# Two transformer blocks in one kernel: the list scheduler places by its timeline simulator

## The chip, the cores and the metric

The kernel runs on one core of a Trainium2 chip. The metric is the device time of one execution in microseconds (us); the time before is the median of three runs.

## The reference

A sequence of 512 tokens of width 1024 goes through a first block and then, with 16 meta tokens put in front (528 tokens), through a second block of two layers. All is fp32.

- First block: `h = rms_norm(x)`, a projection `h @ w_in`, three kinds of attention on it (banded with dilations 1, 4 and 16; a sliding window with sinks; stick-breaking), three gated branches merged and `@ w_out`, a residual; then `gelu(conv(h @ w_up)[gate]) * conv(h @ w_up)[value] @ w_down` with 4096 hidden columns, a residual.
- Second block, twice: `h += 0.5 * swiglu(rmsnorm(h))` with 2816 hidden columns; a mixer of four retention heads and four differential attention heads (softmax in blocks of 128 queries), `@ w_out`; `h += 0.5 * swiglu(rmsnorm(h))` again. At the end a norm, and the 512 tokens go out.

## The kernel before

**Products.** Every large product is made of three matmuls for one: weights and activations are split into a high part (fp32r, `H`) and a rest (`L`), and `H*yH + H*yL + L*yH` is added up in PSUM (`gemm`, L172; `gemm_pairs`, L206; `v_direct`, L579). The blocks of gate and up weights go through seven half-size products instead of eight (`strassen`, L276 for a product that opens a PSUM bank, L278 for one that adds to it).

**Weights.** A raw block of 128 x 1024 (512 KB) comes by a DMA from SP's queue (`wraw`, L153, three buffers). ACT casts it to the high part and DVE subtracts (`wsplit`):

```python
self.nc.scalar.copy(out=H, in_=raw)
self.nc.vector.tensor_sub(out=L, in0=raw, in1=H.bitcast(F32))
```

(L139 and L140) into `wqH` and `wqL`, four buffers of 1024 columns each. So a weight goes raw buffer, ACT, DVE, TensorE, and each step waits until its buffer is free. For the seven products DVE makes sums of the raw quarters first (L258 to L263).

**Stages.** In the profiled execution, by the code's order: norm, attention A and C (to about 240 and 380 us), attention B with the gate products, the merge of the branches (`merge`, L933 to L937; its 24 gate tiles are read back from DRAM by DMAs on ACT's queue; to about 515), `w_out` and the norms (to 575), the convolution FFN (to about 1030), then the second block: swiglu (to 1490), mixer (to 1720 with `w_out`), swiglu, swiglu of the second layer (to 2525), mixer (to 2740), last swiglu (to 3119), the end.

**Attention steps.** A softmax goes TensorE, DVE, ACT, TensorE, ACT, TensorE: scores (in the mixer L1467 to L1470), maximum on DVE (L1472, L1477), exponent on ACT (L1479), normalization on DVE, transposes on TensorE (L1497, L1501), their copies on ACT (L1498, L1502), products with V (L1504, L1505). `diff_heads` staggers three such blocks by Python generators.

**What sets the order.** The kernel's Python code issues instructions in an order of its own, the program order, and opens pools of tiles with fixed numbers of buffers. When the `TileContext` closes, a list scheduler walks through a simulated time: whenever an engine (or a DMA queue) is free in it, that engine is given the instruction that is earliest in program order among those whose inputs and buffers are ready at that simulated time. Each engine then executes its list strictly in order on the chip, with semaphores wherever one engine needs another's result. Counted in the built program, TensorE's 21,605 matmul instructions follow program order except at 852 places, which all lie in the attention, merge and norm stages; in the long feed-forward stretches there is none. DVE's and ACT's lists interleave evacuations of PSUM with weight splits nearly everywhere.

## Time and profile before

| | |
|---|---|
| median of 3 runs | 3139.04 us (3138.15 to 3143.01) |
| the profiled execution, its own time | 3133.03 us |
| its span, first to last instruction | 3131.2 us |
| TensorE busy | 3101.2 us, 99% |
| DVE busy, ACT busy | 2250.4 us, 72%; 1534.7 us, 49% |
| mean granted clock of TensorE | 0.996 |

The profiled execution lies 6.0 us under the median, and its own time is 1.8 us over its span. A matmul's record is longer than its share of the array (records of neighbours overlap), so the pace of a stretch is its length over its count, and not the mean of the records.

### The profile page before, as it was taken

How to read it: one execution, taken by the hardware profiler on the slowest of the kernel's cores; microseconds unless marked ns; L12 is line 12 of the kernel's file. 1: busy time of each engine (PE TensorE's matmuls, PEld its weight loads, DVE VectorE, ACT ScalarE, POOL GpSimd, SP SyncE). 2: the span in 40 equal slices, each digit the busy share in tenths (PEclk: the TensorE clock that was granted, in tenths of full speed). 3: DMA queues.
4: the chain of work that ended last, by engine and by line, in shares of the span. 5: the costliest groups of instructions: out<-in, count | busy, mean ns of one | idle time of the engine just before them, and what ended most of it. 6: DMA issues, size and time to landing. Idle time of an engine off the chain costs nothing.

```text
span 3131.2 us, 54851 instructions
## 1 busy us (share of the span) xinstructions
PE 3101.2 (99%) x22264; PEld 2869.7 (92%) x22264; DVE 2250.4 (72%) x4225; ACT 1534.7 (49%) x2968; POOL 30.9 (1%) x64
## 2 busy tenths in 40 slices
PE   8999999999999999999999999999999999999998
PEld 6876798989898999999889999999999988899998
DVE  6256677977878887775866877768777586687775
ACT  5346556655555554444643544444444464354443
POOL 1000000000000000000000000000000000000000
PEclk9999999999999999999999999999999999999999
DMA  6121256323233422332112232322323311223232
GB/s 212 60 66 60 89 166 202 105 88 102 101 108 101 135 78 93 102 118 87 52 55 78 82 102 89 101 95 95 102 94 111 100 58 62 71 82 108 95 108 75
DMA packets 96958, 304.41 MB, mean 97 GB/s; under 512 B 12199, under 2 KB 20799, under 8 KB 96576
## 3 DMA queue, kind: packets, MB, share of 16 engines
q1 hardware_dynamic: 90384, 286.63, 27.8%
q0 software_dynamic: 2720, 7.78, 0.8%
q10 hardware_dynamic: 3600, 6.49, 0.7%
q8 instruction: 174, 2.85, 0.4%
q14 instruction: 80, 0.66, 0.1%
HBM read 290.34 MB, written 14.45 MB: 97 GB/s over the span
## 4 chain that ended last, share of the span: by engine, by line
PE 95%; DMA 2%; DVE 1%; ACT 1%; issue 0%; ACTq 0%; SPq 0%; DVEq 0%
PE ps_g L172 35%; PE ps_g L278 18%; PE ps_g L276 9%; PE ps_s L172 8%; PE ps_g L206 7%; PE ps_o L276 5%; PE ps_g L579 2%; PE ps_o L206 1%; DMA tmp_p<-gates 1%; PE ps_s L1468 1%; PE ps_s L513 1%; PE ps_o L535 1%; PE ps_s L1525 1%; PE ps_o L1504 1%; PE ps_o L1534 1%; PE ps_t L494 1%
## 5 line engine op out<-in xcount | busy, mean ns | idle before, releaser
L140 DVE TENSOR_TENSOR wqL<-wraw,wqH 128x512 fp32r<-128x512 f32 (+1 forms) x676 | 604.9, 910 | 278.2 <-ACT wqH L139 270.7
L139 ACT CAST wqH<-wraw 128x512 fp32r<-128x512 f32 (+1 forms) x676 | 527.1, 796 | 511.2 <-PE ps_g L172 282.5
L172 PE MATMUL ps_g<-yL,wqH 128*128 128x264 f32 (+2 forms) x1520 | 429.7, 320 | 0.4 <-DVE yL L414 0.4
L172 PE MATMUL ps_g<-yH,wqH 128*128 128x264 f32 (+2 forms) x1520 | 429.6, 321 | 0.0
L172 PE MATMUL ps_g<-yH,wqL 128*128 128x264 f32 (+2 forms) x1520 | 429.0, 321 | 0.3 <-DVE wqL L140 0.2
L278 PE MATMUL ps_g<-t,wqH 128*128 128x256 f32 (+1 forms) x1760 | 326.5, 283 | 0.0
L172 PEld LDWEIGHTS ps_g<-yL,wqH 128*128 128x128 f32 x1520 | 264.1, 189 | 23.7 <-issue 4.2
L172 PEld LDWEIGHTS ps_g<-yH,wqH 128*128 128x128 f32 x1520 | 262.6, 189 | 21.6 <-issue 3.1
L172 PEld LDWEIGHTS ps_g<-yH,wqL 128*128 128x128 f32 x1520 | 262.4, 189 | 21.0 <-issue 2.6
L278 PEld LDWEIGHTS ps_g<-t,wqH 128*128 128x128 f32 x1760 | 272.3, 188 | 1.8
L278 PE MATMUL ps_g<-t,wqL 128*128 128x256 f32 (+1 forms) x880 | 248.4, 282 | 0.0
L139 ACT CAST wqH<-ws 128x1024 fp32r<-128x1024 f32 x100 | 105.2, 1052 | 126.4 <-PE ps_o L276 33.6
L278 PEld LDWEIGHTS ps_g<-t,wqL 128*128 128x128 f32 x880 | 165.9, 189 | 0.0
L276 PE MATMUL ps_g<-t,wqH 128*128 128x264 f32 (+1 forms) x800 | 148.5, 283 | 0.0
L172 PE MATMUL ps_s<-hL,wqH 128*128 128x264 f32 (+1 forms) x544 | 141.2, 317 | 0.0
L172 PE MATMUL ps_g<-hL,wqH 128*128 128x264 f32 (+1 forms) x544 | 141.2, 317 | 0.0
L172 PE MATMUL ps_g<-hH,wqL 128*128 128x264 f32 (+1 forms) x544 | 141.1, 317 | 0.0
L172 PE MATMUL ps_s<-hH,wqL 128*128 128x264 f32 (+1 forms) x544 | 141.1, 317 | 0.0
L172 PE MATMUL ps_g<-hH,wqH 128*128 128x264 f32 (+1 forms) x544 | 141.0, 317 | 0.0
L172 PE MATMUL ps_s<-hH,wqH 128*128 128x264 f32 (+1 forms) x544 | 140.9, 316 | 0.0
L258 DVE TENSOR_TENSOR ws<-wraw 128x512 f32<-128x512 f32 x100 | 69.2, 692 | 86.1 <-DMA wraw<-in_ffn_w_gate 34.8
L140 DVE TENSOR_TENSOR wqL<-ws,wqH 128x1024 fp32r<-128x1024 f32 x100 | 122.4, 1224 | 6.3 <-ACT wqH L139 2.6
(445 smaller groups left out, 8234.8 us busy)
## 6 DMA issues: line engine op xcount, KB each, us to landing
wraw<-in_ffn_w_gate SPq DMA_DIRECT2D x88, 512.0 KB, 3.6
wraw<-in_ffn_w_up SPq DMA_DIRECT2D x88, 512.0 KB, 3.6
wraw<-in_ffn_w_down SPq DMA_DIRECT2D x88, 512.0 KB, 3.5
wraw<-in_w_in SPq DMA_DIRECT2D x86, 512.0 KB, 3.7
wraw<-in_w_up SPq DMA_DIRECT2D x64, 512.0 KB, 3.7
wraw<-in_w_down SPq DMA_DIRECT2D x32, 512.0 KB, 3.5
wraw<-in_w_gate SPq DMA_DIRECT2D x24, 512.0 KB, 4.1
tmp_p<-gates ACTq DMA_DIRECT2D x24, 256.0 KB, 3.3
```

What stands on the lines that cost most here:

```text
L139: self.nc.scalar.copy(out=H, in_=raw)
L140: self.nc.vector.tensor_sub(out=L, in0=raw, in1=H.bitcast(F32))
L172: self.nc.tensor.matmul(t[:, :m], lhsT=a, rhs=b[:, o:o + m], start=(k == 0 and i == 0), stop=(k == nk - 1 and i == 2))
L206: self.nc.tensor.matmul(q[:, :m], lhsT=a, rhs=b[:, o:o + m], start=(k == 0 and i == 0), stop=(k == nk - 1 and i == 2))
L258: nc.vector.tensor_add(out=S[:, :512], in0=A21, in1=A22)
L276: nc.tensor.matmul(ps, lhsT=a, rhs=b, start=first, stop=last)
L278: nc.tensor.matmul(ps, lhsT=a, rhs=b, start=False, stop=last, skip_group_check=True)
L494: nc.tensor.transpose(pt[:, s * P:(s + 1) * P], p[:, s * P:(s + 1) * P], self.ident)
L513: nc.tensor.matmul(ps[:, c], lhsT=q[:, i * P:(i + 1) * P], rhs=k[:, lo * P:(i + 1) * P], start=True, stop=True)
L535: nc.tensor.matmul(ops[obase:obase + 64, i * P:(i + 1) * P], lhsT=V(kb), rhs=pT[:, s0:s0 + P], start=(kb == lo), stop=(kb == i))
L579: nc.tensor.matmul(ps[:, :256], lhsT=a[:, ts], rhs=w, start=(k == 0 and i == 0), stop=(k == KD - 1 and i == 2))
L1468: nc.tensor.matmul(ps[:nq, :e - a], lhsT=qm[r], rhs=k[2][r, a:e], start=False, stop=not dg)
```

## The change

The scheduler's simulated time comes from another machine model. So far it was a simple model of each instruction's duration; now it is the library's timeline simulator, which follows each engine's parts, queues and transfers event by event. The rule of the list scheduler, the instructions, the numbers of buffers and the transfers stay; what can differ is the order of each engine's list and, with it, which instruction gets which buffer and when a transfer is issued.

```diff
-    with tile.TileContext(nc) as tc:
+    with tile.TileContext(nc, schedule_with_timeline_sim=True) as tc:
         build(tc, A)
```

## Rows read from the trace of the kernel before

**Rows 1.** Busy time of the engines over the whole span, from the page.
```profile
PE 3101.2 (99%) x22264; PEld 2869.7 (92%) x22264; DVE 2250.4 (72%) x4225; ACT 1534.7 (49%) x2968; POOL 30.9 (1%) x64
```

**Rows 2.** Busy time by stage: length; PE, PEld, DVE, ACT, POOL; clock, DMA share, GB/s.
```profile
0.00:8.36 8.36, 0.00 (x0) 0.00 (x0) 1.93 (x10) 3.19 (x5) 2.37 (x9) 1.00 0.72 218
...
38.17:60.00 21.83, 17.66 (x111) 16.02 (x111) 11.61 (x17) 8.96 (x19) 2.48 (x5) 0.84 0.70 246
60.00:240.00 180.00, 179.67 (x885) 138.73 (x886) 68.66 (x98) 74.56 (x175) 12.68 (x25) 0.97 0.20 63
240.00:455.00 215.00, 213.30 (x1271) 171.32 (x1270) 153.45 (x375) 122.45 (x271) 8.50 (x16) 1.00 0.31 100
455.00:575.00 120.00, 116.44 (x788) 106.52 (x787) 86.28 (x174) 68.83 (x139) 0.00 (x0) 1.00 0.59 188
575.00:1490.00 915.00, 914.72 (x6667) 868.58 (x6665) 716.77 (x1179) 471.55 (x786) 0.00 (x0) 1.00 0.30 100
1490.00:1720.00 230.00, 228.77 (x1671) 202.64 (x1671) 158.82 (x460) 111.24 (x307) 0.00 (x0) 1.00 0.18 61
1720.00:2525.00 805.00, 804.62 (x6569) 800.87 (x6568) 594.08 (x1007) 374.91 (x654) 0.00 (x0) 1.00 0.30 97
2525.00:2740.00 215.00, 214.97 (x1381) 181.49 (x1380) 146.71 (x395) 102.68 (x269) 0.00 (x0) 1.00 0.19 62
2740.00:3119.00 379.00, 378.43 (x2800) 359.62 (x2799) 282.22 (x459) 174.42 (x308) 0.00 (x0) 1.00 0.29 94
3119.00:3131.20 12.20, 2.79 (x16) 2.21 (x15) 4.51 (x12) 1.05 (x3) 0.00 (x0) 0.62 0.25 86
```

**Rows 3.** Waits of TensorE over the span: total us, times, longest.
```profile
PE ps_g L172 <- ACT oH L323: 8.4, 1, 8.4
PE ps_g L579 <- DVE qk L563: 4.2, 1, 4.2
PE ps_g L206 <- DVE tmp_p L937: 2.4, 3, 1.1
PE ps_s L1467 <- ACT tmp_P L1479: 0.3, 1, 0.3
```

**Rows 4.** Two pieces of the chain that ended last: start, us, count.
```profile
614.71 5.55 PE ps_g L172 x24
...
1810.13 5.82 PE ps_g L278 x48
```

**Rows 5.** One period of the convolution FFN and one of a swiglu, columns as Rows 2.
```profile
610.45:673.82 63.37, 63.37 (x398) 56.93 (x398) 51.30 (x76) 37.96 (x59) 0.00 (x0) 1.00 0.31 102
...
1801.36:1833.48 32.12, 32.12 (x266) 32.12 (x266) 23.96 (x37) 14.29 (x23) 0.00 (x0) 1.00 0.25 83
```

**Rows 6.** Timeline of a swiglu: one weight split and its later use.
```profile
1799.86 1.06 ACT L139 CAST wqH<-ws 128x1024 fp32r<-128x1024 f32 x1 [0.16 <-PE ps_o L276]
...
1800.98 1.22 DVE L140 TENSOR_TENSOR wqL<-ws,wqH 128x1024 fp32r<-128x1024 f32 x1
...
1808.50 0.40 PE L276 MATMUL ps_g<-t,wqH 128*128 128x264 f32 x2
```

**Rows 7.** TensorE in two stretches at a lower granted clock: length, busy (count), clock.
```profile
40.00:50.00 10.00, 7.65 (x30) 0.66 0.87 296
...
205.00:215.00 10.00, 10.00 (x21) 0.56 0.17 54
```

**Rows 8.** Timeline of TensorE in the second of them.
```profile
207.07 3.78 PE L791 MATMUL ps_s<-rows,sel 4*128 4x512 f32 x4
```

**Rows 9.** Groups of instructions on ACT in the mixers' softmax.
```profile
L1479 ACT ACTIVATE tmp_P<-ps_s,sm 128x264 f32<-128x264 f32 (+4 forms) x88 | 40.3, 460 | 28.5 <-DVE sm L1477 23.3 <-DVE sm L1485 4.2 <-PE ps_s L1470 0.5
...
L1502 ACT COPY tmp_aT<-ps_o 16x128 f32<-16x128 f32 (+1 forms) x36 | 8.5, 236 | 3.1 <-PE ps_o L1501 2.9
```

**Rows 10.** The merge's transfers: queue, count, KB, us to landing.
```profile
tmp_p<-gates ACTq DMA_DIRECT2D x24, 256.0 KB, 3.3
```

**Rows 11.** Weight loads of `gemm` on TensorE, one group of three alike.
```profile
L172 PEld LDWEIGHTS ps_g<-yL,wqH 128*128 128x128 f32 x1520 | 264.1, 189 | 23.7 <-issue 4.2
```

## The prediction

> **What bounds the kernel now.** I read the page's busy times first, then the same times cut into stages, then TensorE's waits, then the chain's pieces for the pace. TensorE is busy 3101.2 of 3131.2 us [rows 1], so 30.0 us of the span are all that it ever stands idle. The stages say where [rows 2]: 8.4 us before the first matmul, 4.2 us in the stretch from 38 to 60, 0.3 + 1.7 + 1.2 + 0.0 = 3.3 us in the four attention stretches (60 to 240, 240 to 455, 1490 to 1720, 2525 to 2740), 3.6 us in merge and `w_out` (455 to 575), 0.3 + 0.4 + 0.6 = 1.2 us in the three feed-forward stretches, 9.4 us in the last 12.2 us: together 30.1, rounded. The named waits are the same ones [rows 3]: the first matmul on the first split input (8.4), the first V product on an evacuation (4.2), the merge on its gate products (2.4), and of all the softmax steps of the mixers one wait of 0.3 us.
>
> A busy TensorE can still be slow, so I check the pace. A 264-column matmul takes 5.82 / 48 = 0.1213 us and a 512-column one 5.55 / 24 = 0.231 us in stretches that nothing interrupts [rows 4]. A swiglu period holds 266 matmuls in 32.12 us, or 0.1208 each [rows 5]: by the code 2 x 84 matmuls of the seven products and 2 x 48 of the down projection, 264 x 0.1213 = 32.0 us. So the feed-forward stretches, 915 + 805 + 379 = 2099 us [rows 2], run at the pace of the instruction, with nothing between, and an order cannot make a matmul shorter.
>
> **The change part by part.** Nothing is added or removed; every engine keeps its instructions. So the cost is what the new lists do to TensorE's idle time and to its clock, stage by stage, against the profiled execution's own 3133.03 us.
>
> *Feed-forward stretches, 2099 us.* TensorE's list here is program order already, and always has a ready matmul, so I expect the same list. What may move is DVE's and ACT's mix of evacuations and weight splits. The cover is the lead of the splits: a buffer is freed by TensorE at 1799.7 (the cast starts 0.16 us later), the split is complete at 1800.98 + 1.22 = 1802.2, and its first matmul starts at 1808.5 [rows 6]: 6.3 us ahead, five DVE splits of 1.22 us. A swap of neighbours on DVE costs an evacuation of some 0.4 us or a split of 1.2 us; neither reaches 6.3. DVE itself is busy 51.3 of 63.4 us in the tightest period [rows 5], so 12 us of waits per period would have to be added before it set the pace. Cost 0; bounds -1.2 (all idle gone) and, if the cover went, +1 us for each of the 7 convolution periods of 63.4 us, +7.
>
> *Start, 8.4 us.* The DMA engines are busy 0.72 of it at 218 GB/s [rows 2], for x and the first weights, and SP's list is short here: one raw block more ahead of x would cost 512 KB / 218 GB/s = 2.4 us, one fewer would give back as much. Taken: 0; bounds -2.4 and +2.4.
>
> *38 to 60 us.* [...] Taken: -1; bounds -7.6 and, if it is no better placed and the wait doubles, +4.2.
>
> *Attention stretches, 840 us.* Here TensorE's list is the scheduler's own work: it fills the time of each softmax with matmuls of neighbouring products, and so well that 3.3 us are left. The gain is bounded by these 3.3 us and one clock drop: over 205 to 215 the clock reads 0.56 [rows 7], 8.8 us at half speed, up to 4.4 us lost, while TensorE worked on L791, matmuls of only 4 rows, near 0.9 us each (3.78 / 4) [rows 8]. Another spacing of these twelve might avoid it, or lengthen it. The loss has more room. The mixers have 36 softmax blocks (the copy x36), and where ACT stood idle before the exponent it mostly waited for DVE's scaled maximum, 23.3 us over 88 exponents [rows 9], or 0.26 each. TensorE hides all that today. If the new list puts its filling matmuls earlier, and a third of the blocks (12) then leaves TensorE waiting for two exponents of 0.46 us and two such idles of 0.26, that is 12 x 1.4 = 17 us; all 36 give 52. I take a tenth of the blocks, 4 x 1.4 = +6, nearer the row of today's single wait of 0.3 us [rows 3] than the far end; bounds -7.7 and +52.
>
> *Merge and `w_out`.* ACT's queue issues the 24 gate loads of 3.3 us each [rows 10], behind whatever ACT executes; the sigmoid, DVE's product and the freeing of a PSUM bank wait for each. Three waits of TensorE come of it now [rows 3]. Twice as many would be +2.4; none, with the norm's gaps closed too, -3.6. Taken: 0.
>
> *The end, 9.4 us idle.* It is a dependent chain from the last matmul over sum, norm and the last output transfers; no order shortens it. Cost 0.
>
> Sum: 0 + 0 - 1 + 6 + 0 + 0 = +5 on 3133.03, so 3138 for an execution like the profiled one; against the median, which lies 6.0 us higher, 3139.04 + 5 = 3144 us. I do not trust the sign of a sum of -1 and +6, but the place of the largest term I do.
>
> The TensorE's clock, told by rows: it fell to half once behind the idle 4.2 us and once under the 4-row matmuls. [...]
>
> **The rivals.**
>
> *Slower, by uncovered softmax blocks.* A third to all of the 36 blocks, as priced: +17 to +52, that is 3156 to 3191 us. For it: TensorE's list in these 840 us is remade by the change, and the present one leaves nothing to gain. Against it: ACT is busy 49% and DVE 72%, so a product's matmuls are nearly always there to fill with, and the mixers' one wait shows how much cover there is. It decides from about 9 uncovered blocks on.
>
> *Faster, by gaps and clock.* The 4.2 us wait, both clock drops, and half of the small gaps of attention and merge: 4.2 + 3.4 + 4.4 + 3.5 = 15.5, so 3123.5 us. For it: each of these hangs on one place in a list, and the new model follows queues and transfers. Against it: several must fall together to be seen at all.
>
> *Faster, by hidden stalls.* TensorE's loads are busy only 138.7 + 171.3 + 202.6 + 181.5 = 694 of the 840 us of attention [rows 2]. If that meant that TensorE stalls inside its records there, up to 146 us could be won, 2993 us. Against it: a load takes 189 ns [rows 11], and behind a 512-column matmul that paces at 231 ns [rows 4] it fills only 82% of a saturated stretch; 82% of 840 us are 689, just what is read. [...]
>
> *No change of any order that matters.* Program order decides ties in both models; if readiness falls alike, all lists are nearly the same and the time is 3139.
>
> **How the numbers follow.** 0.2% (6.3 us) is about what a measurement of this kernel can tell from no change. My own case, small gaps traded in the attention stretches (-6 to +10 us; 3133 to 3149), holds 0.44, and 0.33 of it lies within 0.2%, 0.11 above. Lists that change nothing 0.08, all within. Uncovered softmax blocks 0.27, all slower. Faster by gaps and clock 0.19, faster by hidden stalls 0.02: 0.21. So faster 0.21, same 0.41, slower 0.38. For eight in ten I go from the middle of the faster case down to the bounds without the start, 3139 - 1.2 - 7.6 - 7.7 - 3.6 = 3119, to the upper rival without its last quarter, 3183. My likeliest case alone is 3133 to 3149.
>
> **What would show it.** Right: TensorE busy within 10 us of 3101, the swiglu period at 32.1 us with 266 matmuls, the first wait near 8.4 us, differences only in rows of 38 to 60, attention and merge. The step on attention is wrong if waits of L1467, L1497 or L1504 on ACT or DVE add up to more than 10 us, or if those stretches get shorter by more than 8. The step on the feed-forward stretches is wrong if a period is longer than 32.1 or 63.4 us or if TensorE waits for `wqL`. The forecast as a whole is wrong if DVE's list puts evacuations of later products ahead of splits for 6 us or more, or if SP's queue stands behind a buffer that is freed later than before.

## The result, and the profile after

The changed kernel takes 3263.86 us (median of 4 runs, 3260.58 to 3267.16), against 3138.6 us for the kernel before in the same comparison (3137.31 to 3143.01): a ratio of 1.0397, 95% interval 1.0379 to 1.0415. It is 125 us slower, and the predicted range ended at 3183 us.

The profiled execution of the changed kernel took 3265.32 us. Its page's busy times, as [rows 1]:

```profile
PE 3174.3 (97%) x22264; PEld 2924.9 (90%) x22264; DVE 2243.5 (69%) x4225; ACT 1548.7 (47%) x2976; POOL 31.0 (1%) x64
```

The span is 3263.5 us, 132.3 longer (more than the 125 of the medians, because the profiled execution before lay 6.0 us under its median). Of these, 59.2 are new idle time of TensorE (3263.5 - 3174.3 = 89.2, before 30.0), and 73.1 are more time recorded as busy, for the same 22264 instructions. DVE's and ACT's work is what it was to within 1%.

To compare stages I cut the trace after where TensorE has started as many matmuls as at the cuts of [rows 2]. Length; PE, PEld, DVE, ACT, POOL; clock, DMA share, GB/s:

```profile
8.36:53.15 44.79, 44.47 (x233) 35.54 (x233) 35.24 (x57) 28.24 (x49) 6.36 (x12) 1.00 0.70 242
53.15:233.66 180.51, 177.46 (x886) 141.14 (x884) 68.18 (x98) 68.24 (x167) 13.78 (x27) 0.97 0.24 77
233.66:500.41 266.75, 234.80 (x1272) 186.04 (x1270) 153.34 (x382) 130.10 (x287) 8.51 (x16) 0.88 0.25 80
500.41:624.86 124.45, 119.67 (x789) 108.78 (x788) 84.79 (x167) 67.02 (x136) 0.00 (x0) 0.97 0.56 185
624.86:1561.29 936.43, 922.47 (x6666) 875.65 (x6665) 717.71 (x1185) 474.98 (x789) 0.00 (x0) 0.99 0.30 98
1561.29:1823.37 262.08, 255.22 (x1672) 219.77 (x1671) 162.10 (x460) 115.51 (x309) 0.00 (x0) 0.87 0.16 53
1823.37:2628.94 805.57, 805.05 (x6568) 801.80 (x6567) 585.73 (x1004) 379.09 (x658) 0.00 (x0) 1.00 0.30 97
2628.94:2872.26 243.32, 234.25 (x1381) 194.49 (x1379) 149.63 (x395) 104.36 (x268) 0.00 (x0) 0.89 0.17 55
2872.26:3251.41 379.15, 378.24 (x2801) 359.55 (x2800) 280.17 (x462) 177.20 (x310) 0.00 (x0) 1.00 0.29 94
```

Three stages carry the loss: the first block's attention from 240 us (266.75 against 215, +51.8), mixer 0 (+32.1) and mixer 1 (+28.3). The stage of the convolution FFN is +21.4, merge and `w_out` +4.5. The second stretch of swiglu is +0.6 and the last one +0.2; the stretch up to the 232nd matmul is 6.9 us shorter.

Each of the two mixers now holds one stretch of time at half clock that has no counterpart before, and the first block's attention holds a third:

```profile
394.00:435.00 41.00, 30.83 (x118) 23.47 (x119) 16.56 (x76) 16.36 (x54) 0.00 (x0) 0.50 0.13 42
1647.00:1715.00 68.00, 62.48 (x215) 43.14 (x215) 35.03 (x138) 29.74 (x110) 0.00 (x0) 0.50 0.02 8
2711.00:2760.00 49.00, 44.59 (x145) 29.19 (x143) 22.13 (x78) 18.13 (x69) 0.00 (x0) 0.51 0.00 1
```

In mixer 0 TensorE makes 215 matmuls in 68 us, 0.32 us each, at a granted clock of 0.50 throughout. DVE is busy half of it, and the DMA engines almost never (0.02): hardly any weight is being used. The product matmuls (L172 alone) of mixer 0 after show why; length, PE, PEld, clock, DMA share, GB/s:

```profile
1570.00:1580.00 10.00, 8.91 (x65) 8.17 (x65) 1.00 0.32 107
1580.00:1590.00 10.00, 8.56 (x63) 7.98 (x64) 1.00 0.04 11
...
1640.00:1650.00 10.00, 3.18 (x20) 2.37 (x18) 0.83 0.31 106
1650.00:1660.00 10.00, 0.00 (x0) 0.00 (x0) 0.50 0.00 1
...
1700.00:1710.00 10.00, 0.00 (x0) 0.00 (x0) 0.50 0.00 0
1715.00:1725.00 10.00, 9.63 (x79) 9.37 (x77) 1.00 0.03 6
```

The same view of the kernel before, in its mixer 0:

```profile
1510.00:1520.00 10.00, 6.94 (x44) 5.74 (x45) 1.00 0.16 50
...
1560.00:1570.00 10.00, 5.32 (x28) 3.90 (x29) 1.00 0.23 85
1580.00:1590.00 10.00, 5.62 (x30) 4.21 (x31) 1.00 0.00 1
1600.00:1610.00 10.00, 9.68 (x78) 9.51 (x79) 1.00 0.11 36
```

Before, 28 to 44 product matmuls per 10 us were spread among the softmax steps as long as these lasted, and 78 came once they were over. After, more than 60 come at the start, and then the softmax steps stand alone. What the clock does to one of them, the product with V: duration in ns, least, median, most, before and then after.

```profile
L1504 PE MATMUL ps_o<-vh,tmp_aT x160: 271/275/377, 1505.7 to 2619.1; 128*128 128x128 f32 x160
```
```profile
L1504 PE MATMUL ps_o<-vh,tmp_aT x160: 270/418/583, 1596.0 to 2758.6; 128*128 128x128 f32 x160
```

After, the 40 of them that start from 1663.6 to 1703.3 us, at a clock of 0.50, have a median of 421 ns, and the 25 from 2645.2 to 2699.9 us, at 1.00, a median of 275.

TensorE's waits after, as [rows 3]: total us, times, longest.

```profile
PE ps_g L172 <- ACT oH L323: 8.7, 1, 8.7
PE ps_o L535 <- ACT tmp_pT L497: 7.6, 10, 1.1
PE ps_s L904 <- issue: 6.7, 1, 6.7
PE ps_s L904 <- DVE ca L901: 6.3, 1, 6.3
PE ps_t L1426 <- ACT vh L1427: 6.1, 4, 2.3
PE ps_s L364 <- DVE rc L353: 3.9, 5, 1.5
```

But for the first, which stood there before, they are steps of attention and norm, many and short; none of TensorE's waits in this view is for a DMA. The named waits explain only part of the loss, because 73 of the 132 us are recorded as busy and are not gaps.

The steady periods of the convolution FFN and of swiglu, found in the trace after by matmul count, as [rows 5]:

```profile
729.12:792.24 63.12, 63.12 (x398) 56.81 (x397) 51.79 (x78) 32.93 (x50) 0.00 (x0) 1.00 0.30 97
1904.64:1936.76 32.12, 32.12 (x266) 32.12 (x265) 24.13 (x38) 14.37 (x24) 0.00 (x0) 1.00 0.29 96
```

The swiglu period is as long as before, and the steady period of the convolution FFN is 0.25 us shorter for the same matmuls (63.12 against 63.37). The 21.4 us of that stage lie elsewhere: the matmuls fall 5 us behind over the first 25 us of it (625 to 650), and another 17 between 1084 and 1191, around the norm that ends the convolution FFN. TensorE's named waits in those 107 us add up to 10.5 us, the longest for the last hidden activations (`hH`, L1092, 3.7 us) and for the split output of the norm (`yL` and `yH`, L413 and L414, 3.3 us).

### The profile page after: what moved, and what is told of

The parts are those of the page before. It is cut to its first block, busy times and chain, and to the rows that moved or that the text cites. A ratio compares the mean times of both kernels' runs of the same rounds, so it can differ in the third digit from the quotient of the medians.

```text
span 3263.5 us, 54955 instructions
## 1 busy us (share of the span) xinstructions
PE 3174.3 (97%) x22264; PEld 2924.9 (90%) x22264; DVE 2243.5 (69%) x4225; ACT 1548.7 (47%) x2976; POOL 31.0 (1%) x64
## 4 chain that ended last, share of the span: by engine, by line
PE 93%; DVE 2%; ACT 2%; DMA 1%; issue 1%; DVEq 0%; ACTq 0%; SPq 0%
PE ps_g L172 35%; PE ps_g L278 18%; PE ps_g L276 9%; PE ps_s L172 8%; PE ps_g L206 7%; PE ps_o L276 4%; PE ps_g L579 2%; PE ps_s L1468 1%; PE ps_o L1504 1%; PE ps_o L206 1%; PE ps_o L535 1%; DMA tmp_p<-gates 1%; PE ps_s L1467 1%; PE ps_s L1525 1%; PE ps_o L1505 1%; PE ps_o L1534 1%
## 5 line engine op out<-in xcount | busy, mean ns | idle before, releaser
L140 DVE TENSOR_TENSOR wqL<-wraw,wqH 128x512 fp32r<-128x512 f32 (+1 forms) x676 | 596.8, 907 | 263.6 <-ACT wqH L139 259.6
L139 ACT CAST wqH<-wraw 128x512 fp32r<-128x512 f32 (+1 forms) x676 | 515.9, 797 | 541.5 <-PE ps_g L172 228.1
L172 PE MATMUL ps_g<-yH,wqH 128*128 128x264 f32 (+2 forms) x1520 | 434.7, 324 | 4.9 <-ACT yH L413 3.1
L172 PE MATMUL ps_g<-yL,wqH 128*128 128x264 f32 (+2 forms) x1520 | 432.3, 321 | 3.9 <-DVE yL L414 3.8
L172 PE MATMUL ps_g<-yH,wqL 128*128 128x264 f32 (+2 forms) x1520 | 434.3, 322 | 0.9 <-DVE wqL L140 0.9
L172 PEld LDWEIGHTS ps_g<-yH,wqH 128*128 128x128 f32 x1520 | 267.9, 192 | 26.6 <-issue 3.7
L172 PEld LDWEIGHTS ps_g<-yL,wqH 128*128 128x128 f32 x1520 | 269.2, 192 | 24.3 <-DVE yL L414 4.7
L172 PEld LDWEIGHTS ps_g<-yH,wqL 128*128 128x128 f32 x1520 | 268.7, 191 | 21.8 <-issue 1.9
L172 PE MATMUL ps_s<-hH,wqH 128*128 128x264 f32 (+1 forms) x544 | 145.4, 317 | 0.0
L172 PE MATMUL ps_g<-hH,wqH 128*128 128x264 f32 (+1 forms) x544 | 145.2, 317 | 0.0
L172 PE MATMUL ps_g<-hL,wqH 128*128 128x264 f32 (+1 forms) x544 | 141.3, 317 | 0.0
L172 PE MATMUL ps_g<-hH,wqL 128*128 128x264 f32 (+1 forms) x544 | 141.3, 317 | 0.0
L172 PE MATMUL ps_s<-hL,wqH 128*128 128x264 f32 (+1 forms) x544 | 141.0, 317 | 0.0
L172 PE MATMUL ps_s<-hH,wqL 128*128 128x264 f32 (+1 forms) x544 | 141.0, 316 | 0.0
L258 DVE TENSOR_TENSOR ws<-wraw 128x512 f32<-128x512 f32 x100 | 69.1, 691 | 89.7 <-DMA wraw<-in_ffn_w_up 42.5
```

Source lines behind the costliest of these rows:

```text
L172: self.nc.tensor.matmul(t[:, :m], lhsT=a, rhs=b[:, o:o + m], start=(k == 0 and i == 0), stop=(k == nk - 1 and i == 2))
L258: nc.vector.tensor_add(out=S[:, :512], in0=A21, in1=A22)
```

## The experiments

**The theory.** The list scheduler gives an engine an instruction as soon as the simulated engine can take one. The timeline simulator has a setting for each engine, its window: so many instructions may be given to the simulated engine ahead of their execution. The simple model has none. The windows are settings of the scheduler's model, and the runs below change them; how far ahead the chip's own engines are fed, no run here shows. The theory says: with a long window to fill, and few softmax steps ready at that moment, the scheduler commits product matmuls, which are always ready; a softmax step that becomes ready meanwhile stands behind them. In the trace after, DVE's normalization L1490 is complete a median of 3.5 us before TensorE starts the transpose L1497 in this phase of mixer 0 (before: 0.74 us; from the starts and ends of both in the timelines). So the chains run late and the fillers run out. Counted in the built programs, matmuls that stand in runs of 25 or more attention matmuls with no product between are 98 before and 457 after. Theory A is that TensorE's list, made so, is the loss. Its rivals: DVE's and ACT's lists; or the simulator's durations.

**The window.** Six kernels differ from the changed one in these settings alone, made ahead of the `TileContext`: the windows named below, with the others as they come. The first has TensorE's window at 2.

TensorE 2:

> [...] Theory A (TensorE's window: the list scheduler commits matmuls of later products up to 35 instructions, some 4 us, ahead of the array, so that softmax steps that become ready meanwhile stand behind them, the matmuls are used up too early, and the last softmax blocks run bare): 3139 us within 15, the time at half clock down from 221 us to under 40, no bare stretch in attention C, attention B and the mixers. Rival B (ACT's and DVE's lists delay the softmax steps): still over 3230 us. Rival C (the simulator's softmax chain takes longer in its time than the simple model's, whatever the window): still over 3230 us.

TensorE 70:

> The suspected cause doubled: TensorE's window in the simulator is 70 instead of 35. Theory A: the bare stretches grow. In the list itself the runs of 25 or more attention matmuls with no product between hold 730 instructions, against 503 in the changed kernel; 125 us of loss times 730/503 give 181, so about 3320 us (3290 to 3360). Rivals B and C: 3264 us within 15.

TensorE's as it comes, ACT and DVE 2:

> ACT's and DVE's windows in the simulator are 2 instead of 12, TensorE's stays 35. Theory A: the bare runs in TensorE's list hold 480 instructions instead of 503, so 3250 us within 20. Rival B: most of the loss is gone, 3139 to 3180 us. Rival C: 3264 us within 15.

All three 2:

> All three windows are 2. Theory A: as with TensorE's window alone, 3139 us within 15, the difference to it within 8 us. Rival B: clearly below the run with TensorE's window alone, by 50 us or more. Rival C: still over 3230 us.

TensorE 12:

> TensorE's window 12, between 2 (3161 us) and 35 (3264 us). The runs of 25 or more attention matmuls with no product between hold 249 instructions in this list, against 56 at 2 and 457 at 35, counted alike. Theory A, in proportion: 3161 + 103 x (249 - 56) / (457 - 56) = 3211 us, within 15. If a window of any length costs the same once it is there: 3264 us within 15.

TensorE 4:

> The changed kernel with TensorE's window at 4 instead of 35. In the built list 28 matmuls stand in runs of 25 or more attention matmuls with no product between, in one run (55 with a window of 2, 98 before, 249 with 12, 457 with 35). Theory A (the long bare runs make the loss; what is left at a window of 2 is something else): 3161, like a window of 2, 3150 to 3170. Rival B, loss grows with the window by itself: between the windows of 2 and 12, 3170 or more. Faster than before (under 3132) would need that the simulator's times are better than the simple model's once the window is right; I give that one chance in ten.

Measured. Idle and busy are TensorE's in each profiled execution, less those of before (30.0 and 3101.2 us). The time at half clock is (1 - mean clock) x 2 x span; the clock records of the traces before and after hold 1.00 and 0.50 alone. Bare is the count of matmuls in runs as above (the 503, 730 and 480 of two of the expectations were counted otherwise; alike they are 457, 672 and 434). Each ratio is to the kernel before in the same comparison, whose median was 3136.36 to 3139.17 us.

| kernel | median us | ratio, interval | bare | idle | busy | half clock |
|---|---|---|---|---|---|---|
| before | 3138.6 | 1 | 98 | 0 | 0 | 25 |
| TensorE 2 | 3160.94 | 1.0077, 1.0063 to 1.0091 | 55 | +18.9 | +10.4 | 57 |
| all three 2 | 3159.28 | 1.0072, 1.0060 to 1.0085 | 55 | +15.4 | +10.9 | 57 |
| TensorE 4 | 3164.95 | 1.0087, 1.0071 to 1.0102 | 28 | +18.8 | +12.6 | 57 |
| TensorE 12 | 3200.12 | 1.0195, 1.0175 to 1.0214 | 249 | +33.2 | +35.0 | 128 |
| ACT, DVE 2 | 3252.97 | 1.0374, 1.0359 to 1.0388 | 434 | +55.6 | +63.8 | 208 |
| the change | 3263.86 | 1.0397, 1.0379 to 1.0415 | 457 | +59.2 | +73.1 | 228 |
| TensorE 70 | 3310.79 | 1.0561, 1.0545 to 1.0577 | 672 | +80.2 | +105.0 | 312 |

The time follows TensorE's window in both directions, with the durations of the simulator untouched. A window of 2 takes away about 100 of the 125 us; ACT's and DVE's windows alone about 10. The windows of 70, 12 and 4 and the one of ACT and DVE fall within the ranges of theory A. The window of 2 misses its range by some 7 us at the upper end, and its half clock too (57 us against under 40); with all three at 2 the miss is 5 us. What is left there comes back below. A window of 4 has fewer bare matmuls than one of 2 and is not faster, and the kernel before has 98 and is the fastest, so below some 100 the count decides nothing any more. The same stages of the kernel with TensorE's window at 2:

```profile
236.79:461.71 224.92, 218.66 (x1272) 175.21 (x1270) 151.49 (x375) 121.84 (x271) 8.50 (x16) 0.98 0.30 95
580.39:1507.85 927.46, 918.29 (x6666) 871.41 (x6666) 714.48 (x1185) 474.28 (x789) 0.00 (x0) 0.99 0.31 99
1507.85:1747.05 239.20, 232.97 (x1672) 204.92 (x1671) 158.49 (x460) 111.26 (x307) 0.00 (x0) 0.97 0.18 58
...
2556.14:2769.62 213.48, 212.13 (x1379) 180.86 (x1380) 146.23 (x395) 101.72 (x266) 0.00 (x0) 1.00 0.20 63
```

Mixer 1 is back at the length of [rows 2] (213.48 against 215). The first block's attention keeps +9.9, the stage of the convolution FFN +12.5, mixer 0 +9.2.

**Whose list?** Five kernels pin lists. A helper ties TensorE's matmuls, each behind the one before it, in the order that another kernel's built program has; the scheduler then places only the rest. (Pinned to its own order, the kernel before keeps every list as it was.)

```diff
+def pin(tc):
...
+    pe = [i for i in tc.nc.cur_bb.bb.instructions
+          if i.engine == mybir.EngineType.PE and "Matm" in type(i).__name__]
+    order = [pe[k] for k in np.cumsum(steps) - 1]
...
+    for a, b in zip(order, order[1:]):
+        tc.add_manual_dep(b, a.name, info, reason="pin")
...
         build(tc, A)
+        pin(tc)
```

The simple model, with TensorE in the order of the changed kernel:

> The opposite crossing: the simple model schedules, but TensorE's matmuls are pinned to the order that they have in the changed kernel. Theory A: 3264 us within 20, with the four bare stretches at half clock. Rival B: well under 3230 us, because ACT's and DVE's lists are those of the simple model.

Measured: 3281.69 us, 1.0459 (1.0440 to 1.0479). The new order of TensorE is enough for the whole loss and 18 us more, with DVE and ACT placed by the old model.

The timeline simulator, with TensorE in the order of before:

> The changed kernel, scheduled by the timeline simulator with its windows as they are, but TensorE's matmuls are pinned to the order that they have in the kernel before. All other lists (ACT, DVE, the DMA queues) and the buffers are the timeline simulator's. Theory A (the loss lies in TensorE's list alone): 3139 us within 10. Rival B (the other lists carry a part, such as the 22 us that were left with the short window): 3155 us or more.

Measured: 3271.14 us, 1.0424 (1.0407 to 1.0440). Here theory A falls as I had stated it: TensorE's old order does not save the time when the other lists are new. TensorE's waits in that kernel:

```profile
PE ps_t L345 <- DVE tmp_acc L338: 42.5, 8, 10.4
PE ps_s L1467 <- ACT tmp_P L1479: 12.5, 12, 2.5
PE ps_t L494 <- DVE tmp_p L530: 10.3, 4, 6.4
```

TensorE stands up to 10.4 us, 42.5 in all, for DVE's last sum of a norm; in the kernel before that wait came once, for 1.5 us.

Only the matmuls issued inside the mixers pinned to the order of before, the rest free:

> The changed kernel with the old TensorE order pinned only inside the two mixers. By the ledger of matched matmuls the mixers carry 32 + 29 of the loss, the rest lies in the first block and around the norms. Theory A with an additive ledger: 3264 - 61 = 3203 us within 12. If the loss is given back elsewhere, or the bare stretch only moves behind the mixer: over 3230 us.

Measured: 3237.31 us, 1.0320 (1.0304 to 1.0336): 27 us back where 61 were expected, on the side of the second bound. Each mixer keeps somewhat under half of its loss (13.9 of 32.1 and 13.1 of 28.3 us), with 11.6 us of waits for the exponent in 12 pieces. The half clock is nearly gone from them; columns as [rows 2]:

```profile
1564.13:1808.05 243.92, 233.35 (x1672) 205.29 (x1671) 160.72 (x460) 111.00 (x307) 0.00 (x0) 0.99 0.18 57
2614.69:2842.76 228.07, 220.31 (x1381) 185.27 (x1379) 148.49 (x394) 101.74 (x268) 0.00 (x0) 0.98 0.18 59
```

So I asked whether the windows of DVE and ACT make their lists misfit the old order, and set both to 2 in the kernel with TensorE in the order of before, and then TensorE's to 2 as well:

> Timeline simulator, TensorE's matmuls pinned to the order of the kernel before, and in the simulator ACT's and DVE's windows cut from 12 to 2; nothing of the computation changes. Theory A (committed work ahead on ACT and DVE puts weight splits and evacuations in front of the norm and softmax steps that TensorE's old order needs soon; this made the 132 us of the run with the pinned order and full windows): most of it goes, 3139 to 3170 us. Rival B (the simulator's own durations and latencies, and not the windows of ACT and DVE, make their lists misfit the old order): the loss stays above half, 3205 us or more.

> The same, and TensorE's window 2 too. With TensorE's order pinned its window can only move simulated times by a little. Theory A: within 10 us of the run with ACT's and DVE's windows at 2. Rival B, that TensorE's window sets when ACT's and DVE's inputs seem ready and so their lists too: at least 20 us faster than that run.

Measured: 3215.41 us (1.0242, 1.0222 to 1.0261) and 3208.55 us (1.0225, 1.0208 to 1.0242). The windows of ACT and DVE account for some 56 of the 132 us; the remaining 76 lie on rival B's side of the bound. TensorE's window matters little once its order is pinned. Without the pin and with the same three windows the time was 3159.28, so an order of TensorE that is excellent with its own lists costs 49 us beside lists that were made with another model's times. In the first of the two kernels the wait for the norm's last sum is halved and still the largest that is new:

```profile
PE ps_t L345 <- DVE tmp_acc L338: 19.1, 7, 5.6
PE ps_g L172 <- ACT oH L323: 8.6, 1, 8.6
PE ps_s L1467 <- ACT tmp_P L1479: 7.4, 11, 1.5
```

Change of each stage's length against [rows 2], in us, all cut by matmul count:

| stage of before | change | simple, new order | timeline, old order | TensorE 2 |
|---|---|---|---|---|
| 0 to 60 | -6.9 | -5.5 | +3.8 | -6.3 |
| 60 to 240 | +0.5 | +0.5 | +3.3 | +3.1 |
| 240 to 455 | +51.8 | +54.3 | +21.5 | +9.9 |
| 455 to 575 | +4.5 | +9.0 | +9.1 | -1.3 |
| 575 to 1490 | +21.4 | +21.5 | +23.6 | +12.5 |
| 1490 to 1720 | +32.1 | +32.9 | +25.6 | +9.2 |
| 1720 to 2525 | +0.6 | +8.8 | +25.6 | +4.1 |
| 2525 to 2740 | +28.3 | +26.3 | +11.0 | -1.5 |
| 2740 to 3119 | +0.2 | +5.9 | +15.5 | +0.2 |

The change and the simple model with the new order agree within 3 us in every attention stage: with the new order of TensorE it is that order that sets the time there, whichever of the two models made the other lists. The pinned old order loses by another way, 65 of its 138 us in feed-forward stretches where the change loses 22.

**Too short a window.** All three windows at 1:

> All three windows at 1, so that no engine can be given an instruction ahead of time at all. The built list has again 457 matmuls in bare runs of 25 or more, but in 11 runs of at most 68 (the changed kernel: four of 64, 86, 162 and 145). Theory A by the number of matmuls in bare runs: 3264 us, plus or minus 20. Theory A by length (only what a run has beyond some 50 matmuls counts: 64 and 68 here, so 32 of 257 beyond 50): 3139 + 125 x 32 / 257 + 22, or 3177, plus or minus 15. Rival B (a shorter window is better, whatever the runs): 3161 or less.

Measured: 3745.69 us, 1.1931 (1.1912 to 1.1950). All three expectations fall. The bare runs are not what decides here: 324 of the 613 us of the longer span lie in the three feed-forward stretches, where TensorE now waits, as for the next sums of activations and the evacuations of the seven products:

```profile
PE ps_g L278 <- DVE gu L301: 63.1, 18, 8.0
PE ps_s L364 <- DVE rc L353: 49.3, 14, 11.0
PE ps_t L345 <- DVE tmp_acc L338: 41.5, 12, 10.0
PE ps_g L278 <- ACT cu L287: 24.6, 10, 4.8
```

It refutes that a shorter window is better as such, and says nothing on whether bare runs count by number or by length.

## Why the prediction was wrong

**The failed step is the attention term**: "I take a tenth of the blocks, 4 x 1.4 = +6", nearer to the one wait of 0.3 us than to the bound of +52. The attention stages measured +0.5 + 51.8 + 32.1 + 28.3 = +113, above even the upper bound. Three things were wrong in it.

First, the argument about cover. "ACT is busy 49% and DVE 72%, so a product's matmuls are nearly always there to fill with": the busy share of the other engines says nothing on this. What covers a softmax is a stock of product matmuls, and a list can spend that stock early; after the change it did, and from 1650 to 1712 us mixer 0 had 6 of them left. The rival "uncovered softmax blocks" named this mechanism ("if the new list puts its filling matmuls earlier") and had a chance of 0.27; the runs with the window show that it is the main one. It was too small as well: it gave 3156 to 3191 us.

Second, the price. I priced an uncovered block as two exponents and two idles of ACT, 1.4 us, one block beside the other, at full clock. After, the two slow stretches in the mixers hold the normalization (L1490) of 19 of the 36 blocks; length, DVE on L1490 (count), clock, DMA share, GB/s:

```profile
1647.00:1715.00 68.00, 5.66 (x11) 0.50 0.02 8
2711.00:2760.00 49.00, 4.49 (x8) 0.51 0.00 1
```

The mixers lost 32.1 + 28.3 = 60.4 us, or 3.2 for each of these 19. In them the busy time grew more than the idle time: 255.22 - 228.77 = 26.5 us against 5.6, and 234.25 - 214.97 = 19.3 against 9.0. How much of the busy time is the clock can only be estimated: the records of L1504 went from 275 to 418 ns, so about a third of the 30.83 + 62.48 + 44.59 = 137.9 us that TensorE is busy in the three slow stretches, some 47 us, would go at full clock. Over the span that stands beside +73.1 us busy and +59.2 idle, and in every kernel of the window table with more than 100 bare matmuls the busy time grows by 0.34 to 0.37 us for each us more at half clock. The prediction counted two drops of the clock, both from the trace before, and no new one. In that trace the clock reads 0.50 from 43.1 to 49.9 us, behind the 4.2 us wait, and in the trace after a stretch recorded as 92% busy (62.48 of 68 us) sat at 0.50 from end to end; what makes the granted clock fall and rise was not shown.

Third, the extent. The upper bound of +52 counted the 36 blocks of the mixers alone. For the attention of the first block no loss was priced (of L791 it says only that another spacing might lengthen the drop), and its part from 240 to 455 us is the stage that lost most, +51.8 us. There the idle time is the larger part, 31.95 - 1.70 = 30.3 us against 21.5 of longer busy time, and the waits are those of its own steps (L535 for the copy L497, 7.6 us; L904 for its chain on DVE, 6.3 + 3.9 us).

The sign that the prediction had set for this step, waits of L1467, L1497 and L1504 on ACT or DVE of more than 10 us, did not show it: in the view of [rows 3] they add up to 8.2 us after. A sign made of waits misses what is recorded as busy.

**Feed-forward stretches, cost 0.** The cost holds for the periods: the one of swiglu is unchanged, the one of the convolution FFN 0.25 us shorter, and two of the three stretches are within 0.6 us. The reason given for it does not: "I expect the same list". Counted in the built programs, TensorE's list after the change leaves program order some 15 times in every 300 matmuls of these runs of periods, where it never did before; the time of the periods hardly moves all the same. The stage from 575 to 1490 is outside its bounds (+21.4 against +7), because I treated it as one run of periods and never priced the norms, the one at its start and the one that ends the convolution FFN, where the matmuls fall behind.

**Start and 38 to 60 us.** Taken -1 with a bound of -7.6 (the 4.2 us wait and 3.4 for the clock behind it) for the second; the stretch to the 232nd matmul got 6.9 us shorter. The first wait stayed (8.7 us), the second went, and the clock behind it stayed up (1.00 from 8.36 to 53.15, where TensorE is idle for 0.32 us): the one gain that the rival "faster, by gaps and clock" had right. No run shows the 3.4 us that the bound and this rival count for the clock there; the runs showed a clock of 0.66 over 40 to 50 us before, and 1.00 over the stretch after.

**Merge and `w_out`.** Taken 0, upper bound +2.4; measured +4.5, of which the clock is part: it reads 0.86 over the last 25 us of the stage.

**The end.** 12.09 against 12.20 us: right.

**Faster, by hidden stalls.** No run bears it out. The weight loads' share fell from 92% to 90% as the time rose by 4%, in the direction that such a reading would give, but the cause is bare stretches and not stalls inside records. The argument against it, 82% of 840 us, came out by luck: it takes 512-column products throughout, while in the mixers the products have 264 columns, and such a swiglu period has its loads busy for all of its 32.12 us [rows 5].

**What stays open.** About 22 us of the 125 remain with a window of 2, in the norms, mixer 0 and the first block. The largest new waits there are those for a norm's steps (L364 for DVE 7.3 us in 10 pieces, L345 3.0) and one of 2.9 us for a normalization in a mixer (L1497 for L1490); which of the simulator's assumptions beside the window makes them was not separated. Why lists of ACT and DVE made with windows of 2 still cost 76 us beside the old order of TensorE is open for the same reason. No version that beats the kernel before was found.

## What to carry to other kernels

Where a list scheduler fills the gaps of dependent chains with independent work, ask how many instructions ahead its model may commit: each filler committed ahead is put in front of a chain step, and when the stock of fillers is gone the chains stand bare. The shortest window is no remedy: with all windows at 1 the kernel took 3745.69 us. Price a bare stretch as a whole, at half clock if the trace shows the clock to fall there, as it did here to 0.50, and not as a sum of single waits. And do not judge one engine's list by itself: an order taken from one model and put beside lists from another lost more than either model's own set.

## What the runs showed of the hardware

The granted clock stayed at 0.50 for 68 us on end (1647 to 1715 us, after) while TensorE was recorded busy for 62.5 of them, with 215 matmuls, nine in ten of them of the attention. A 128x128 fp32 matmul of L1504 went from a median of 275 to 418 ns over the whole span, 1.5 times; after, it was 421 in a stretch at 0.50 and 275 in one at 1.00. A loss of 4% showed little in TensorE's busy share, which went down only from 99% to 97%; the mean granted clock, 0.996 to 0.965, was the plainer sign.
